# Mixture-of-experts layers: TensorE's work for a pair of experts in three blocks in a fixed order, its sums one pair later

## The chip, the cores and the metric

The kernel runs on one NeuronCore of a Trainium2 chip. Its time is the device time of one launch in microseconds (us), the median over several runs. The profile is of one further execution of the same program.

## The reference

A network of one block and then two layers, on 256 tokens of 1024 numbers. The change touches only the mixture of experts (MoE) that closes each of the two layers. It has 16 experts in 4 groups; each token goes to two experts:

```
p_group = softmax(tok @ w_router_group); grp = argmax(p_group)
top_p, top_i = top_k(softmax(logits of that group's 4 experts), 2)
weight = p_group[grp] * top_p / sum(top_p)
...
for an expert e and its tokens:  y = (silu(tok @ w1[e]) * (tok @ w3[e])) @ w2[e]     # w1, w3: 1024x512, w2: 512x1024
...
x = x + gate * (sum over a token's two experts of weight * y)
```

One layer's weights w1, w3, w2 are 16 x 6 MB = 96 MB in float32; they are read from HBM once per layer.

## The kernel before

The program is written with a tile framework: the code names tiles and operations, and a scheduler decides the order in which each engine takes its instructions, by its own model of their times, unless the code sets it. Each engine then runs its list strictly in order and waits where an operand is not ready.

`moe(layer)` computes a layer's experts in eight **pairs**. Every expert has 64 places for tokens (CAP), so the two experts of a pair share the 128 columns of TensorE's array: expert i=0 uses columns 0 to 63, i=1 columns 64 to 127. A pair's work, with the lines of the kernel before:

- *first products* `ph` (L1644): 32 matmuls on half the columns, c=0 for w1 and c=1 for w3, alternating between the two halves of the array;
- `h` = silu of the first (L1649, ScalarE) times the second (L1664, VectorE), then four transposes to `hT` (L1669), copied out by VectorE and ScalarE (L1671);
- the *combine matrix* `ct` (L1655) and the routing weights `ws` (L1657), from `dm`, which says which token has which place;
- *output products* (L1679): 16 matmuls on half the columns, n=0 and n=1 for the two halves of the 1024 outputs;
- y = output x `ws` x gate (L1696, VectorE), split into a high part `yh` (L1697, ScalarE) and a low part `yl` (L1698, VectorE);
- the *sums* into four accumulators `macc` in PSUM (L1556, in `flush`): eight matmuls on the full array for a pair;
- for every second pair, `dispatch`: two comparisons on VectorE make the next two pairs' `dm` (L1490), and 32 matmuls on the full array (L1496) gather their tokens to `xg`, which ScalarE and VectorE copy out of PSUM (L1502, L1500).

The lines that make a pair's half-array work:

```
for k in range(KC):
    for i in range(2):
        pe.matmul(ps[64 * i:64 * i + 64], xg[:, k, CAP * i:CAP * i + CAP],
                  r3(w[4 * c + 2 * (k // 4) + i], 4)[:, k % 4], start=k == 0, stop=k == KC - 1)
...
fi = [(f, i) for f in range(4) for i in range(2)]
for f, i in sorted(fi, key=lambda v: v[1]) if (pr, n) == (7, 1) else fi:
    pe.matmul(ps[64 * i:64 * i + 64], hT[:, f, 64 * i:64 * i + 64], w2[n][i][:, f], start=f == 0, stop=f == 3)
```

A float32 matmul stands in the trace as two records, so 32 matmuls are 64 records.

Weights come as 1 MB tiles `mw`, twelve to a pair, 96 to a layer, by SP's DMA queue in order. There are 19 places for them; the first 19 of a layer are loaded ahead, during the work before it (L1388), the other 77 as places come free (L1421). Tiles in PSUM come from a pool `pa` of four banks; the other four hold `macc`. Before the last pair stands a branch (`overflow`, L1564 and L1565), which is entered only if an expert has more than 64 tokens; every engine passes it, and nothing of the last pair is ahead of it on TensorE. The last three weight tiles of a layer are issued behind it.

Of the kernel before, what the change touches and what calls it, by code (L numbers as in the profile page):

```python
# [48 lines left out]
def body(tc, A, out, stop=None, start=None):  # L49
# [1375 lines left out]
    def moe(layer):  # L1425
# [5 lines left out]
        def tl(shape, name, bufs=1, dt=F32):  # L1431
            return cur[-1].tile(shape, dt, name=name, tag=name, bufs=bufs)
# [48 lines left out]
        def dispatch(pr):  # L1481

            me, cur[-1] = cur[-1], md
            dm = tl([P, 2, 4, CAP], "dm", dt=F32R)
            xg = tl([P, KC, 4 * CAP], "xg")
            cur[-1] = me
            for i in range(2):
                ready.append((dm.bitcast(F32)[:, :, 2 * i:2 * i + 2], xg[:, :, 2 * CAP * i:2 * CAP * (i + 1)]))
            for b in range(2):
                dve.tensor_tensor(dm[:, b], iota[:, None, 1:CAP + 1].to_broadcast([P, 4, CAP]),  # L1490
                                  po[:, b, 2 * pr:2 * pr + 4, None].to_broadcast([P, 4, CAP]), op=ALU.is_equal)
            for k in range(KC):
                ps = pa([P, 4 * CAP])
                for b in range(2):
                    for x_ in (xnh, xnl):
                        pe.matmul(ps, x_[:, b, k * P:(k + 1) * P], fl(dm[:, b]), start=b == 0 and x_ is xnh,  # L1496
                                  stop=b == 1 and x_ is xnl)
                o = xg[:, k]
                if k % 2:
                    dve.tensor_scalar(o, ps, a[:, k:k + 1], b_[:, k:k + 1], op0=ALU.mult, op1=ALU.add)  # L1500
                else:
                    act.activation(o, ps, AF.Identity, scale=a[:, k:k + 1], bias=b_[:, k:k + 1])  # L1502
                if k == 3:
                    yield
            yield

        ready, md = [], cur[-1]
        xnh, xnl = tl([P, 2, D], "xnh", dt=F32R), tl([P, 2, D], "xnl", dt=F32R)
        for n in range(2):
            ns = slice(512 * n, 512 * n + 512)  # L1510
            for b in range(2):
                act.mul(xnh[:, b, ns], x[:, b, ns], rsx[:, b:b + 1])
                dve.scalar_tensor_tensor(xnl[:, b, ns], x[:, b, ns], rsx[:, b:b + 1], xnh[:, b, ns].bitcast(F32),
                                         op0=ALU.mult, op1=ALU.subtract)
        for _ in dispatch(0):
            pass

        p8 = el.rearrange("p b e g -> p b (e g)").rearrange("p b (s k) -> p b s k", s=2)
        sm, wk = tl([P, 2, 4], "rsm"), tl([P, 2, 2], "wk")
# [9 lines left out]
        wt = tl([P, 2, 16], "wt")  # L1529
        dve.tensor_mul(oe, oe, wk[:, :, :, None].to_broadcast([P, 2, 2, 16]))  # L1530
        dve.tensor_add(wt, oe[:, :, 0], oe[:, :, 1])
        def hy():

            return tl([P, 512], "h")

        def add(b, c, ps, i):

            o = x[:, b, c:c + ps.shape[-1]]
# [10 lines left out]
        def flush():  # L1549

            while late:
                pr, n, ct, ys = late.pop()
                for y_ in ys:
                    for b in range(2):
                        end = pr == 7 - n and y_ is ys[-1]
                        pe.matmul(acc[b][n], ct[:, b * P:(b + 1) * P], y_, start=pr == 0 and y_ is ys[0], stop=end)  # L1556
                        if end:
                            add(b, 512 * n, acc[b][n], n == 0 and 0)
# [69 lines left out]
                                o = x[:, b, 512 * n:512 * n + 512]  # L1628
                                dve.tensor_add(o, o, g_)

        for pr in range(8):
            dm, xg = ready.pop(0)
            nxt = dispatch(pr + 1) if pr % 2 and pr < 7 else iter(())
            w = [mload() for _ in range(8)]
            if pr == 7:
                overflow()
            w2 = [[r3(mload(), 4) for i in range(2)] for n in range(2)]

            ph = []
            for c in range(2):  # L1640
                ps = pa([P, 512], "ph")
# [3 lines that stand above are left out]
                                  r3(w[4 * c + 2 * (k // 4) + i], 4)[:, k % 4], start=k == 0, stop=k == KC - 1)  # L1645
                ph.append(ps)
                if c == 0:
                    h = hy()
                    act.activation(h, ps, AF.Silu)  # L1649
                    flush()  # L1650

                    ps = pa([P, T + 2])
                    d = [fl(dm[:, b]) for b in range(2)]
                    for b in range(2):
                        pe.transpose(ps[:, b * P:(b + 1) * P], d[b], ident)  # L1655
                    for b in range(2):
                        pe.matmul(ps[:, T:T + 2], d[b], wt[:, b, 2 * pr:2 * pr + 2], start=b == 0, stop=b == 1)  # L1657
                    ct, ws = tl([P, T], "ct", dt=F32R), tl([P, 1], "ws", bufs=2)
                    act.copy(ct, ps[:, 0:T])
                    for i in range(2):  # L1660
                        dve.tensor_copy(ws[64 * i:64 * i + 64], ps[64 * i:64 * i + 64, T + i:T + i + 1])
            for j in range(2):
                js = slice(256 * j, 256 * j + 256)
                dve.tensor_mul(h[:, js], h[:, js], ph[1][:, js])  # L1664
            next(nxt, None)
            ps = pa([P, 4, P])
            hT = tl([P, 4, P], "hT")
            for f in range(4):
                pe.transpose(ps[:, f], h[:, f * P:(f + 1) * P], ident)  # L1669
                if f % 2:  # L1670
                    (dve.tensor_copy if f == 1 else act.copy)(hT[:, f - 1:f + 1], ps[:, f - 1:f + 1])  # L1671
            next(nxt, None)

            for n in range(2):
                ps = pa([P, 512])
                fi = [(f, i) for f in range(4) for i in range(2)]

                for f, i in sorted(fi, key=lambda v: v[1]) if (pr, n) == (7, 1) else fi:
                    pe.matmul(ps[64 * i:64 * i + 64], hT[:, f, 64 * i:64 * i + 64], w2[n][i][:, f],  # L1679
                              start=f == 0, stop=f == 3)  # L1680
                if (pr, n) == (7, 1):
                    y = fl(tl([P, 4, P], "hT"))
                    for c in (0, T):
                        cs = slice(c, c + T)
                        dve.scalar_tensor_tensor(y[:, cs], ps[:, cs], ws, gr[:, 512 + c:768 + c], op0=ALU.mult, op1=ALU.mult)  # L1685
                    flush()
                    for c in (0, T):
                        for b in range(2):
                            ps = pa([P, T])
                            pe.matmul(ps, ct.bitcast(F32)[:, b * P:(b + 1) * P], y[:, c:c + T], start=True, stop=True)  # L1690
                            add(b, 512 + c, ps, 1 + c // T)
                    continue
                flush()
                y = hy()
                yh, yl = md.tile([P, 512], F32R, name="yh", tag="yh", bufs=1), tl([P, 512], "yl", dt=F32R)
                dve.scalar_tensor_tensor(y, ps, ws, gr[:, 512 * n:512 * n + 512], op0=ALU.mult, op1=ALU.mult)  # L1696
                act.copy(yh, y)  # L1697
                dve.tensor_sub(yl, y, yh.bitcast(F32))  # L1698
                late.append((pr, n, ct, (yh, yl)))
        esk.close()  # L1700
        esm.close()
        es.close()
# [426 lines left out]
```

## Time and profile before

| | us |
|---|---|
| median of 3 runs | 2102.05 (2101.83 to 2104.94) |
| the profiled execution | 2101.02 |
| its span, first to last instruction | 2099.2 |
| TensorE busy in the span | 1852.7 (88%) |
| MoE of layer 0, first to last product of the pairs | 233.63 |
| MoE of layer 1, the same | 231.52 |

Times below count from the span's start. A row of the timeline gives start, duration, engine (PE is TensorE, DVE VectorE, ACT ScalarE, SPq the DMA queue of SyncE), line, operation, out<-in, shape, count of records, and in brackets how long the engine was idle before it and what ended that. [...] "128\*64" is the part of the array that a matmul uses (rows\*columns).

### The profile page before, as it was taken

Reading aid. Unit: us, or ns where it says so; the run is one execution under the profiler, and the core shown is the slowest. Engines: PE = TensorE matmul, PEld = TensorE weight load, DVE = VectorE, ACT = ScalarE, POOL = GpSimd, SP = SyncE. Lnnn points to the kernel's source line nnn. Section 1 sums busy time; section 2 is a strip of 40 time slices with the busy share of each in tenths; the row PEclk is TensorE's granted clock in tenths of the full one; section 3 lists DMA queues with packets and bytes.
Section 4 is the critical chain, followed back from the end, with each engine's and each line's share of the span. In section 5 each row is a group of like instructions: output and inputs, shape, how many; then the busy total and the mean of one; then the engine's idle time right before and its main releaser. Section 6 shows DMA issues by size and latency. Waiting matters only on the chain. (4 is left out here: it accounts for less than half of the span.)

```text
span 2099.2 us, 27099 instructions
## 1 busy us (share of the span) xinstructions
PE 1852.7 (88%) x9963; PEld 1182.8 (56%) x9963; DVE 1077.3 (51%) x2616; ACT 603.6 (29%) x1232; POOL 448.7 (21%) x407
## 2 busy tenths in 40 slices
PE   7999999989778788787788799979999899989998
PEld 6787897879633233333333398764433699843432
DVE  6635453455857757667665546752112479531212
ACT  4434342344311111212111234721111454311110
POOL 2100000002544444354444200010000255200000
PEclk9999999999899999999898998989999999999999
DMA  9666644845799999999999774059997372669993
GB/s 317 204 231 195 218 139 146 280 153 170 315 427 426 427 427 427 426 409 427 427 426 427 284 285 161 11 201 401 420 419 313 130 281 91 241 246 419 419 420 119
DMA packets 122678, 624.82 MB, mean 298 GB/s; under 512 B 11534, under 2 KB 16494, under 8 KB 65034
## 3 DMA queue, kind: packets, MB, share of 16 engines
q1 hardware_dynamic: 85675, 354.54, 45.5%
q0 software_dynamic: 36864, 268.45, 30.4%
q8 instruction: 83, 1.36, 0.3%
q14 instruction: 56, 0.46, 0.1%
HBM read 621.80 MB, written 1.16 MB: 297 GB/s over the span
## 5 line engine op out<-in xcount | busy, mean ns | idle before, releaser
L986 PE MATMUL acc<-uv,dg 128*128 128x512 f32 x1024 | 495.3, 642 | 125.3 <-ACT dg L984 125.3
L986 PEld LDWEIGHTS acc<-uv,dg 128*128 128x128 f32 x1024 | 205.1, 205 | 413.6 <-issue 240.2
L974 DVE CUSTOM_DVE_ANT_0 uv<-uv,xn 128x1024 f32<-128x1024 f32 x256 | 316.5, 1240 | 204.1 <-DMA uv<-in_puv,ix 199.0
L973 POOL DMA_INDIRECT uv<-in_puv,ix x256 | 286.2, 1118 | 340.4 <-PE acc L986 236.0
L1644 PE MATMUL ph<-mw,xg 128*64 128x512 f32 x1024 | 256.0, 600 | 4.4 <-PEq L1565 2.7
L142 DVE TENSOR_TENSOR wl<-w,wh 128x1024 fp32r<-128x1024 f32 x129 | 162.9, 1266 | 167.7 <-ACT wh L141 110.3
L141 ACT CAST wh<-w 128x1024 fp32r<-128x1024 f32 x166 | 173.4, 1048 | 248.0 <-PE pb L160 73.9
L1644 PEld LDWEIGHTS ph<-mw,xg 128*64 128x64 f32 x1024 | 77.4, 137 | 145.0 <-issue 139.8
L142 POOL TENSOR_TENSOR wl<-w,wh 128x1024 fp32r<-128x1024 f32 x37 | 90.1, 2438 | 243.4 <-PE pa L270 158.3
L980 ACT ACTIVATE ac<-ac 128x4 f32<-128x4 f32 (+1 forms) x65 | 13.3, 205 | 425.7 <-DVE ac L974 425.6
L159 PE MATMUL pa<-xh,wh 128*128 128x256 f32 x480 | 122.1, 291 | 2.1 <-ACT wh L141 2.1
L1679 PE MATMUL pa<-mw,hT 128*64 128x512 f32 x512 | 123.8, 596 | 0.0
L160 PE MATMUL pa<-xl,wh 128*128 128x256 f32 x480 | 120.1, 287 | 0.0
L159 PEld LDWEIGHTS pa<-xh,wh 128*128 128x128 f32 x480 | 93.6, 195 | 6.4 <-ACT wh L141 3.4
L160 PEld LDWEIGHTS pa<-xl,wh 128*128 128x128 f32 x480 | 93.8, 195 | 0.0
L984 ACT ACTIVATE dg<-cf,ac 128x128 f32<-128x128 f32 x256 | 82.6, 390 | 24.7 <-DVE ac L981 20.2
L160 PE MATMUL pb<-xl,wh 128*128 128x256 f32 x352 | 89.5, 289 | 0.0
L159 PE MATMUL pb<-xh,wh 128*128 128x256 f32 x352 | 89.2, 289 | 0.0
L162 PE MATMUL pa<-xh,wl 128*128 128x256 f32 x480 | 69.1, 288 | 19.7 <-POOL wl L142 15.8
L1679 PEld LDWEIGHTS pa<-mw,hT 128*64 128x64 f32 x512 | 38.9, 136 | 69.0 <-issue 68.2
L1696 DVE SCALAR_TENSOR_TENSOR h<-pa,ws,mgr 128x512 f32<-128x512 f32 x30 | 22.5, 751 | 103.6 <-PE pa L1679 102.6
L162 PEld LDWEIGHTS pa<-xh,wl 128*128 128x128 f32 x480 | 62.4, 194 | 22.2 <-POOL wl L142 16.6
(614 smaller groups left out, 2961.9 us busy)
## 6 DMA issues: line engine op xcount, KB each, us to landing
mw<-in_moe_w SPq DMA_DIRECT2D x192, 1024.0 KB, 14.9
awp<-in_ada_w SPq DMA_DIRECT2D x48, 1024.0 KB, 5.5
w<-in_w_in SPq DMA_DIRECT2D x68, 512.0 KB, 4.7
w<-in_hg_c SPq DMA_DIRECT2D x22, 512.0 KB, 3.8
w<-in_wq SPq DMA_DIRECT2D x16, 512.0 KB, 4.3
w<-in_nsa_c SPq DMA_DIRECT2D x16, 512.0 KB, 8.5
w<-in_w_br SPq DMA_DIRECT2D x8, 512.0 KB, 4.2
w<-in_w_out SPq DMA_DIRECT2D x8, 512.0 KB, 3.5
```

The costliest lines, as they stand in the source:

```text
L141: act.copy(wh[:, :n], w[:, :n])
L142: (lo or dve).tensor_sub(wl[:, :n], w[:, :n], wh[:, :n].bitcast(F32))
L159: pe.matmul(ps, wh[:, k], xh[:, k], start=k == 0, stop=False)
L160: pe.matmul(ps, wh[:, k], xl[:, k], start=False, stop=False)
L162: pe.matmul(ps, wl[:, k], xh[:, k], start=False, stop=k == nk - 1)
L973: pool.indirect_dma_start(w, None, A["puv"], bass.IndirectOffsetOnAxis(ap=ix[b][:, k:k + 1], axis=0))
L974: dve.tensor_tensor_reduce(w[:, 0:D], w[:, 0:D], xn[:, b], 1.0, 0.0, ALU.mult, ALU.add, h[:, s:s + 1])
L984: act.mul(dg, ident, hs[:, i:i + 1])
L986: pe.matmul(acc[b][n], dg, w[:, D + 512 * n:D + 512 * n + 512], start=k == 0, stop=k == P - 1)
L1644: pe.matmul(ps[64 * i:64 * i + 64], xg[:, k, CAP * i:CAP * i + CAP], r3(w[4 * c + 2 * (k // 4) + i], 4)[:, k % 4], start=k == 0, stop=k == ...
L1679: pe.matmul(ps[64 * i:64 * i + 64], hT[:, f, 64 * i:64 * i + 64], w2[n][i][:, f], start=f == 0, stop=f == 3)
L1696: dve.scalar_tensor_tensor(y, ps, ws, gr[:, 512 * n:512 * n + 512], op0=ALU.mult, op1=ALU.mult)
```

## The change

Within a pair TensorE's list is now the written order (`manual_schedule` for that engine alone): the 32 first products; then the full-array work, which is the sums of the pair before, the transposes of `h`, `ct` and `ws`, and every second pair all of `dispatch`; then the 16 output products. The other engines are still ordered by the scheduler. The sums of both halves n of a pair wait for the next pair, so `yh` gets two places, and the low part of n=1 uses the place of `hT`. y is made in PSUM, in the bank of the output product, instead of in `h`.

```
-        for _ in dispatch(0):
-            pass
+        dispatch(0)
...
-                pr, n, ct, ys = late.pop()
+                pr, n, ct, ys = late.pop(0)
...
-        for pr in range(8):
-            dm, xg = ready.pop(0)
-            nxt = dispatch(pr + 1) if pr % 2 and pr < 7 else iter(())
-            w = [mload() for _ in range(8)]
-            if pr == 7:
-                overflow()
-            w2 = [[r3(mload(), 4) for i in range(2)] for n in range(2)]
+        def pair(pr, dm, xg, w, w2):
...
                 if c == 0:
-                    h = hy()
+                    h = tl([P, 512], "h")
                     act.activation(h, ps, AF.Silu)
-                    flush()
-
-                    ps = pa([P, T + 2])
...
             for j in range(2):
                 js = slice(256 * j, 256 * j + 256)
                 dve.tensor_mul(h[:, js], h[:, js], ph[1][:, js])
-            next(nxt, None)
+
+            flush()
             ps = pa([P, 4, P])
             hT = tl([P, 4, P], "hT")
             for f in range(4):
                 pe.transpose(ps[:, f], h[:, f * P:(f + 1) * P], ident)
                 if f % 2:
                     (dve.tensor_copy if f == 1 else act.copy)(hT[:, f - 1:f + 1], ps[:, f - 1:f + 1])
-            next(nxt, None)
+
+            ps = pa([P, T + 2])
+            d = [fl(dm[:, b]) for b in range(2)]
+            for b in range(2):
+                pe.transpose(ps[:, b * P:(b + 1) * P], d[b], ident)
+            for b in range(2):
+                pe.matmul(ps[:, T:T + 2], d[b], wt[:, b, 2 * pr:2 * pr + 2], start=b == 0, stop=b == 1)
...
+            if pr % 2 and pr < 7:
+                dispatch(pr + 1)
...
-                flush()
-                y = hy()
-                yh, yl = md.tile([P, 512], F32R, name="yh", tag="yh", bufs=1), tl([P, 512], "yl", dt=F32R)
-                dve.scalar_tensor_tensor(y, ps, ws, gr[:, 512 * n:512 * n + 512], op0=ALU.mult, op1=ALU.mult)
-                act.copy(yh, y)
-                dve.tensor_sub(yl, y, yh.bitcast(F32))
+
+                yh = tl([P, 512], f"yh{n}", dt=F32R)
+                yl = tl([P, 512], "yl", dt=F32R) if n == 0 else fl(tl([P, 4, P], "hT")).bitcast(F32R)
+                dve.scalar_tensor_tensor(ps, ps, ws, gr[:, 512 * n:512 * n + 512], op0=ALU.mult, op1=ALU.mult)
+                act.copy(yh, ps)
+                dve.tensor_sub(yl, ps, yh.bitcast(F32))
                 late.append((pr, n, ct, (yh, yl)))
+
+        for pr in range(8):
+            dm, xg = ready.pop(0)
+            w = [mload() for _ in range(8)]
+            if pr == 7:
+                overflow()
+            w2 = [[r3(mload(), 4) for i in range(2)] for n in range(2)]
+            with tc.manual_schedule(engines={mybir.EngineType.PE}):
+                pair(pr, dm, xg, w, w2)
```

In the kernel after, first products stand at L1631, output products at L1667, the sums at L1548, transposes at L1645, `ct` at L1652, `ws` at L1654, and the branch at L1557.

TensorE's list of the kernel before, from the output products of pair 1 of layer 0 to the middle of pair 2's second first product (numbers at `macc` are buffer numbers):

```order
L1679 MATMUL pa<-mw,hT 64x512 x16
L1644 MATMUL ph<-mw,xg 64x512 x11
L1556 MATMUL macc_10241<-yh,ct 128x512
L1556 MATMUL macc_10243<-yh,ct 128x512
L1644 MATMUL ph<-mw,xg 64x512
L1556 MATMUL macc_10241<-yl,ct 128x512
L1556 MATMUL macc_10243<-yl,ct 128x512
L1644 MATMUL ph<-mw,xg 64x512 x4
L1655 MATMUL pa<-cf,dm 128x128 x2
L1657 MATMUL pa<-wt,dm 128x2 x2
L1644 MATMUL ph<-mw,xg 64x512 x5
```

Here runs of 11, 1, 4 and 5 half-array matmuls alternate with full-array work. The kernel after, the same pair:

```order
L1631 MATMUL ph<-mw,xg 64x512 x32
L1548 MATMUL macc_10241<-yh_10469,ct 128x512
L1548 MATMUL macc_10243<-yh_10469,ct 128x512
L1548 MATMUL macc_10241<-yl,ct 128x512
L1548 MATMUL macc_10243<-yl,ct 128x512
L1548 MATMUL macc_10242<-yh_10483,ct 128x512
L1548 MATMUL macc_10244<-yh_10483,ct 128x512
L1548 MATMUL macc_10242<-hT,ct 128x512
L1548 MATMUL macc_10244<-hT,ct 128x512
L1645 MATMUL pa<-cf,h 128x128 x4
L1652 MATMUL pa<-cf,dm 128x128 x2
L1654 MATMUL pa<-wt,dm 128x2 x2
```

The 32 first products are one run, and everything on the full array stands behind them; the 16 output products follow.

VectorE's list of the kernel before, pair 1 of layer 0, from the comparisons that make the next `dm` to the copies of `xg`:

```order
L1490 TENSOR_TENSOR dm<-cf,pos 128x256 x2
L1661 COPY ws<-pa 64x1 x2
L1664 TENSOR_TENSOR h<-h,ph 128x256 x2
L1500 TENSOR_SCALAR xg<-pa,ma,mod 128x256 x2
L1671 COPY hT<-pa 128x256
L1500 TENSOR_SCALAR xg<-pa,ma,mod 128x256 x2
```

The same place in the kernel after:

```order
L1639 TENSOR_TENSOR h<-h,ph 128x256 x2
L1647 COPY hT<-pa 128x256
L1490 TENSOR_TENSOR dm<-cf,pos 128x256 x2
L1658 COPY ws<-pa 64x1 x2
L1500 TENSOR_SCALAR xg<-pa,ma,mod 128x256 x4
```

The two comparisons have moved from ahead of the product that makes `h` to behind the copy of `hT`, directly ahead of the copies of `xg`.

## Rows read from the trace of the kernel before

**Rows 1.** Windows: MoE of layer 0, two pairs of it, MoE of layer 1

```profile
1412.31:1645.94 233.63, 224.66 (x1002) 88.36 (x1001) 43.01 (x92) 29.61 (x55) 4.68 (x2) 0.99 0.86 351
1487.06:1544.76 57.70, 56.58 (x262) 23.26 (x261) 11.51 (x24) 7.31 (x14) 0.00 (x0) 1.00 1.01 419
1859.19:2090.71 231.52, 222.81 (x1001) 87.01 (x1000) 42.87 (x90) 27.70 (x53) 0.00 (x0) 1.00 0.85 350
```

**Rows 2.** The chain of waits that ended last: start, us, what

```profile
2065.22 13.89 PE ph L1644 x62
```

**Rows 3.** Waits of TensorE in layer 1's MoE: us in total, times, longest

```profile
PE pa L1669 <- DVE h L1664: 3.0, 5, 0.6
PE pa L1669 <- DVE hT L1671: 2.6, 5, 0.5
PE ph L1644 <- DVEq L1565: 1.7, 1, 1.7
PE pa L1496 <- ACT xg L1502: 0.7, 1, 0.7
PE macc L1556 <- ACT yh L1697: 0.7, 1, 0.7
```

**Rows 4.** Timeline of TensorE, layer 0, pair 1's output products to pair 2's

```profile
1458.88 7.09 PE L1679 MATMUL pa<-mw,hT 128*64 128x512 f32 x32
1465.79 5.31 PE L1644 MATMUL ph<-mw,xg 128*64 128x512 f32 x22
1471.04 0.73 PE L1556 MATMUL macc<-yh,ct 128*128 128x512 f32 x2
1471.70 1.07 PE L1644 MATMUL ph<-mw,xg 128*64 128x512 f32 x2
1472.70 0.74 PE L1556 MATMUL macc<-yl,ct 128*128 128x512 f32 x2
...
1475.23 0.44 PE L1655 MATMUL pa<-cf,dm 128*128 128x128 f32 x2
...
1475.94 2.79 PE L1644 MATMUL ph<-mw,xg 128*64 128x512 f32 x10
1478.66 0.73 PE L1556 MATMUL macc<-yh,ct 128*128 128x512 f32 x2
...
1479.79 5.36 PE L1644 MATMUL ph<-mw,xg 128*64 128x512 f32 x22
1485.76 0.41 PE L1669 MATMUL pa<-cf,h 128*128 128x128 f32 x2 [0.60 <-DVE h L1664]
1486.69 0.44 PE L1669 MATMUL pa<-cf,h 128*128 128x128 f32 x2 [0.52 <-DVE hT L1671]
1487.06 3.65 PE L1679 MATMUL pa<-mw,hT 128*64 128x512 f32 x16
```

**Rows 5.** Timeline of TensorE: matmuls of dispatch, back to back

```profile
1457.01 0.28 PE L1496 MATMUL pa<-dm,xnl 128*128 128x256 f32 x1
1457.13 0.28 PE L1496 MATMUL pa<-dm,xnh 128*128 128x256 f32 x1
```

**Rows 6.** The line of the comparisons for `dm`: ns min/median/max, first and last start

```profile
L1490 DVE TENSOR_TENSOR dm<-cf,pos x16: 417/418/425, 1406.2 to 2000.7; 128x256 fp32r<-128x256 f32 x16
```

**Rows 7.** Timeline of TensorE behind the branch in layers 0 and 1, and pair 7's output

```profile
1614.45 1.28 PE L1644 MATMUL ph<-mw,xg 128*64 128x512 f32 x2 [2.67 <-PEq L1565]
...
2062.43 1.04 PE L1644 MATMUL ph<-mw,xg 128*64 128x512 f32 x2 [1.75 <-DVEq L1565]
...
2081.00 9.71 PE L1679 MATMUL pa<-mw,hT 128*64 128x512 f32 x32
```

**Rows 8.** Windows: layer 0, behind the branch

```profile
1615.00:1622.00 7.00, 7.00 (x20) 3.35 (x20) 1.50 (x4) 0.37 (x1) 0.00 (x0) 0.51 0.97 375
```

**Rows 9.** Timeline of the DMA queue: the streamed weight tiles of layer 0

```profile
1415.99 200.40 SPq L1421 DMA_DIRECT2D mw<-in_moe_w  x77
```

**Rows 10.** Lines of layer 1's MoE: xg's copies (busy us, mean ns, idle before)

```profile
L1502 ACT ACTIVATE xg<-pa,mod,ma 128x256 f32<-128x256 f32 x13 | 7.2, 563 | 18.6 <-PE ph L1644 9.6 <-PE pa L1496 9.0
```

## What the change should do to the time

> **What bounds the kernel now.** I read the windows first. Layer 0's experts take 233.63 us, layer 1's 231.52, together 22% of the span, and TensorE is busy in 224.66 and 222.81 us of them [rows 1]. The end of the chain of waits is matmuls of the last pair [rows 2]. TensorE's waits in layer 1 sum to 8.7 us, those in front of the transposes being the largest [rows 3]. So TensorE sets the pace. The weight stream does not quite: twelve tiles of 1.049 MB to a pair at 419 GB/s are 30.0 us, and two pairs take 57.70, so TensorE eats tiles a little faster than they come, out of the 19 loaded ahead [rows 1].
>
> Busy is not full, and that is what the timeline is for. 32 records (16 half-array matmuls) of output products take 1465.79 - 1458.88 = 6.91 us: 0.432 us each, because the two experts run side by side, 0.864 for two. The single first product at 1471.70 holds the engine until 1472.70: 1.00 us, with nothing on the other half [rows 4]. It counts as busy all the same. Runs of 11, 1, 4 and 5 between full-array work, as the order shows, leave a half empty at each odd end.
>
> **The change part by part.**
>
> *Unit prices, all from [rows 4] unless said.* First products in one run: 32 x 0.432 = 13.8 us. Output products: 6.9. Sums: two of them between half-array work take 1471.70 - 1471.04 = 0.66, four take 1479.79 - 1478.66 = 1.13, so one costs 0.235 and the change to the full array and back 0.19; eight in a row with one change are 2.07. Transposes with the wait for the first copy of hT: 1487.06 - 1485.76 = 1.30. ct and ws: 1475.94 - 1475.23 = 0.71, less the change 0.52. Dispatch: 32 x 0.12 = 3.84 [rows 5].
>
> *What goes.* The wait for the product h, 0.60 in front of the transposes: the eight sums now stand there, 2.07 us, and the two products and their start are 0.6 us behind the last first product, so the cover is ample. It stays in pair 0, which has no sums before it. The odd ends go, six in two pairs by the order (each costs the empty half, 0.43), and seven of nine changes there and back, at 0.19.
>
> *What stays.* The wait between the transposes, 0.52: the second two share a PSUM tile with the copy of the first two. Before, dispatch hid it in odd pairs; now every pair pays it. The branch: 2.67 and 1.75 us before [rows 7]; I take 2.2. Pair 7's last output product keeps its order one expert after the other: 9.71 us instead of 7.09 [rows 7, 4], so 2.6 more.
>
> *What comes.* One new wait, in the three odd pairs of a layer that dispatch. The comparisons for the new dm overwrite what the ws matmuls have just read, so they can't start before these, and dispatch needs them. Before, they lay under first products and nobody waited for them. Each takes 0.42 [rows 6]. From below the wait is 0.42, if the first matmuls need only the first comparison; from above about 1.3, two in a row and a copy ahead of them in VectorE's queue. Dispatch's first two matmuls (0.24) can cover part of the second, so I take 0.8. Behind the comparisons on VectorE stand the ws copies and its copies of xg; nobody needs those within dispatch's own 3.84 us.
>
> *Hidden.* y, yh and yl are read out of PSUM, one step after another, while 13.8 us of the next pair's first products run; a bank of the pool comes round four tiles later, so those products take the banks of hT and ct, not of y. If that cover were gone, two steps of about 0.7 us (yh waited for 0.7 once, [rows 3]) would stand in each pair. The new place of yl, in hT, is free since the output products have read hT, and the next hT is written behind the sums. The weight queue's order is the same.
>
> *The sum for a layer.* Pair 0: 13.8 + 0.6 + 1.30 + 0.7 + 6.9 = 23.3. An even pair: 13.8 + 2.07 + 1.30 + 0.52 + 6.9 = 24.6. An odd pair with dispatch: 24.6 + 3.84 + 0.8 = 29.2, so two pairs 53.8 for 57.70. Pair 7: 24.6 + 2.6 = 27.2. Layer: 23.3 + 3 x 29.2 + 3 x 24.6 + 27.2 + 2.2 = 214.1 us. Against 231.52 layer 1 gains 17.4. Layer 0 would gain 19.5, but 7 us of its 233.63 ran at 0.51 of the clock, at the lower level of 1.2 GHz, behind the 2.67 us in front of the branch [rows 8, 7]; that is 3.4 us, and since a gap of that kind stays, I leave one such drop in and count 16.1. Together 33.5. What follows layer 0 starts as much earlier, and the last additions at the end do the same work: 0.
>
> A check by differences: six odd ends 2.6 and seven changes 1.3, less 0.7 for waits (1.12 before, 1.04 + 0.8 after), are 3.2 us for two pairs, against 3.9 by the sum. With 3.2 the layers give 28 together. I keep 33.
>
> The profiled execution took 2101.02 us, its span 2099.2; the median of the runs is 1.0 above the first. **2102 - 33 = 2069 us.**
>
> **One rule against it.** If only the change of shape cost anything and a half-empty array did not, seven changes at 0.19 less the 0.7 of waits would be 0.6 us for two pairs, some 5 us in all: 2097. The lone matmul of 1.00 us against 0.43 speaks against that. [...]
>
> **The rivals.**
>
> *The clock falls in each pair (slower).* The full-array block now holds the transposes, a wait of 0.52, small matmuls and in odd pairs a wait of 0.8, all at one place, between two dense runs. [...] Against it: the even pairs of before had 0.60 and 0.52 with only transposes between them, and the clock stood at 1.00 over two such pairs [rows 4, 1]. [...]
>
> *The weight stream takes over.* Two pairs need 60 us of stream and would take 53.8. The stream of layer 0 starts at 1416 [rows 9]; its 73rd tile, the last first-product tile of pair 7, is there at about 1416 + 73 x 2.50 = 1598.5 plus the few us that a start takes, say 1603. TensorE would ask for it at 1412.3 + 184.7 + 2.2 + 10.3 = 1609.5. That leaves 6 us. The last three tiles are issued behind the branch, at about 1599, and are asked for from 1616 on. If the stream lost 10 us in each layer, the gain would shrink by 4 each: 2077.
>
> *Late operands.* In a fixed order every operand that is late stops everything. If dispatch, crowded with copies, waits 3 us instead of 0.8 (for banks or for VectorE), six times, the gain falls by 13: 2082. For it: the 0.7 that dispatch once waited for a copy of xg [rows 3]. Against it: a copy takes ScalarE 0.56 us [rows 10], and it has every second one, so one for each 0.96 us of gathering.
>
> *It does nothing.* If scheduler and hardware had in fact overlapped the halves across the breaks, only waits would differ, and by the 0.7 they get worse: 2107. The same row of 1.00 us speaks against it.
>
> **How the numbers follow.** Forecast (2060 to 2077, the clock drops and the dispatch wait within their bounds) 0.72; stream 0.07; late operands 0.09; only the changes of shape count 0.03; nothing, at the upper edge of what counts as the same (within 0.2%, 4 us, about what a measurement of this kernel can tell from no change), 0.05; clock 0.04. The low end is no clock drop at all (-3.4) and the dispatch wait at 0.42 (-2.3), and a little for small waits that vanish: 2060. The high end has drops in both layers (+3.4), the late operands at 13: 2084. Faster is the sum of the first four, 0.91; the fifth is split, so same 0.03, slower 0.06.
>
> **What would show it.** In the trace after, two pairs should be 53.8 us apart; the first products of a pair one row of 64 records in 13.8; eight sums in 2.1; the wait for h only in pair 0; 0.52 between the transposes eight times in a layer; a wait of dispatch for the comparisons, 0.8, three times. The layers should be 214 to 218 us long and the DMA share between 0.9 and 1. I am wrong if first products wait for DMA in pair 7, if the clock is below 1.00 away from the branch, or if the pairs are 57 us apart with the runs unbroken.

## The result, and the profile after

The changed kernel took 2074.40 us (median of 4 runs, 2069.25 to 2081.53), the kernel before 2101.94 on the same chip: a ratio of 0.9858, 95% interval 0.9831 to 0.9884. The forecast was 2069 (2060 to 2084), faster. Run again later, the same kernel took 2067.17 (2064.94 to 2075.62, 5 runs), ratio 0.9846 (0.9823 to 0.9869). The profile below is that of the slowest run, 2081.53, span 2079.7; the profile of the repeat, 2064.94, has the same expert layers, and most of the difference lies in one earlier stage, told at the end.

The windows of both expert layers and of two pairs between them, as in [rows 1] (the stretch A:B and its length in us, then busy time and records of TensorE, its weight loads, VectorE, ScalarE and GpSimd, TensorE's granted clock as a share of full speed, the busy share of the DMA engines, GB/s):

```profile
1424.99:1642.47 217.48, 206.79 (x1002) 87.68 (x1001) 43.95 (x91) 29.69 (x55) 2.69 (x2) 0.99 0.91 377
1495.23:1549.02 53.79, 52.24 (x262) 22.80 (x261) 11.63 (x24) 7.30 (x14) 0.00 (x0) 1.00 1.01 420
1855.06:2072.22 217.16, 206.80 (x1002) 87.73 (x1001) 43.97 (x91) 27.80 (x53) 0.00 (x0) 0.99 0.90 373
```

Layer 0 went from 233.63 to 217.48 us, layer 1 from 231.52 to 217.16, two pairs from 57.70 to 53.79. TensorE does the same matmuls in 16 to 18 us less busy time, which is where the gain is; what is not busy grew, by less than 2 us. Over the two pairs the granted clock is 1.00 and the DMA engines are busy throughout (1.01, 420 GB/s); TensorE has no wait for a weight tile in either layer.

The timeline of TensorE in an even pair of layer 1, to hold against [rows 4]:

```profile
1900.74 7.09 PE L1667 MATMUL pa<-mw,hT 128*64 128x512 f32 x32
1907.66 13.90 PE L1631 MATMUL ph<-mw,xg 128*64 128x512 f32 x64
1921.49 0.74 PE L1548 MATMUL macc<-yh,ct 128*128 128x512 f32 x2
1922.07 0.63 PE L1548 MATMUL macc<-yl,ct 128*128 128x512 f32 x2
1922.54 0.62 PE L1548 MATMUL macc<-yh,ct 128*128 128x512 f32 x2
1923.00 0.62 PE L1548 MATMUL macc<-hT,ct 128*128 128x512 f32 x2
1923.46 0.38 PE L1645 MATMUL pa<-cf,h 128*128 128x128 f32 x2
1924.36 0.44 PE L1645 MATMUL pa<-cf,h 128*128 128x128 f32 x2 [0.52 <-DVE hT L1647]
```

One row of 64 records from start to start takes 1921.49 - 1907.66 = 13.83 us, 0.432 for two; the eight sums 1.97; the wait for `h` is gone and 0.52 between the transposes is left. TensorE's waits in layer 1, which answer to [rows 3] (us in total, times, longest):

```profile
PE pa L1645 <- DVE hT L1647: 4.9, 8, 1.3
PE ph L1631 <- DVEq L1557: 3.3, 1, 3.3
PE pa L1496 <- DVE dm L1490: 1.6, 3, 0.5
PE pa L1645 <- DVE h L1639: 0.6, 1, 0.6
```

`h` is waited for once (pair 0), `hT` in each pair, `dm` in the three pairs that dispatch. Two of these are larger than forecast: the gap at the branch, and one wait for `hT` of 1.3 us. Both belong to pair 7, here in layer 0:

```profile
1613.46 15.65 PE L1631 MATMUL ph<-mw,xg 128*64 128x512 f32 x64 [3.57 <-DVEq L1557]
...
1632.69 0.44 PE L1645 MATMUL pa<-cf,h 128*128 128x128 f32 x2 [1.32 <-DVE hT L1647]
```

Pair 7 waits 3.57 us at the branch, its first products take 15.65 instead of 13.9, and the second transposes wait 1.32 instead of 0.52. The slower first products are explained by a window right behind the branch, where the granted clock is 0.50 for 3.42 us (1.71 us lost, of 15.65 - 13.90 = 1.75):

```profile
1614.15:1617.57 3.42, 3.42 (x10) 1.20 (x8) 0.00 (x0) 0.00 (x0) 0.00 (x0) 0.50 1.01 405
```

### The profile page after: what moved, and what is told of

Read it like the earlier page. It is cut to its first block, busy times and chain, and to the rows that moved or that the text cites. A ratio compares the mean times of both kernels' runs of the same rounds, so it can differ in the third digit from the quotient of the medians.

```text
span 2079.7 us, 27097 instructions
## 1 busy us (share of the span) xinstructions
PE 1833.2 (88%) x9963; PEld 1191.3 (57%) x9963; DVE 1075.7 (52%) x2616; ACT 603.9 (29%) x1232; POOL 449.4 (22%) x407
## 5 line engine op out<-in xcount | busy, mean ns | idle before, releaser
L1631 PE MATMUL ph<-mw,xg 128*64 128x512 f32 x1024 | 226.0, 600 | 6.8 <-DVEq L1557 6.8
L1631 PEld LDWEIGHTS ph<-mw,xg 128*64 128x64 f32 x1024 | 76.1, 138 | 153.3 <-issue 152.2
L1667 PE MATMUL pa<-mw,hT 128*64 128x512 f32 x512 | 116.9, 595 | 0.0
L1639 DVE TENSOR_TENSOR h<-h,ph 128x256 f32<-128x256 f32 x32 | 12.0, 418 | 200.5 <-PE ph L1631 200.5
L1667 PEld LDWEIGHTS pa<-mw,hT 128*64 128x64 f32 x512 | 36.7, 137 | 67.1 <-issue 66.2
```

## The experiments

**The spread.** First the changed kernel once more, with nothing edited.

> The changed kernel once more. Its four runs so far were 2081.5, 2069.3, 2078.5 and 2070.4 us, and its profiled run (2081.5) showed the granted clock at half speed for 6.8 us four times between 320 and 375 us, in a stage that the change does not touch. Theory: two levels, near 2070 and near 2080, told apart by that stage; a profile near 2070 shows 320:375 some 10 us shorter, and 217 us in each expert layer as before. Rival: the spread lies in the expert layers, and they then differ by some 5 us each between a run near 2070 and one near 2080.

Its five runs went from 2064.94 to 2075.62 us. The profiled one (2064.94) has layers of 217.48 and 217.19 us, those of the changed kernel's profile within 0.03, and between 320 and 375 us it is 11 us shorter. So most of the spread is that stage's, as the first theory had it, and the rest lies in other stages ahead of the experts: layer 0 starts 16.0 us earlier in this profile. The two levels are less sharp than the theory said. Its windows stand in the last section.

**Do odd ends cost, and what does a break cost?** Two kernels spread the eight sums among the first products of the next pair, each alone, seven more breaks in each pair from 1 on; only the places differ:

```diff
+            sums = one_by_one()
             ...
                         pe.matmul(ps[64 * i:64 * i + 64], xg[:, k, CAP * i:CAP * i + CAP], ...
+                        if 16 * c + 2 * k + i + 1 in (4, 8, 12, 16, 20, 24, 28, 32):   # even
+                        if 16 * c + 2 * k + i + 1 in (3, 8, 11, 16, 19, 24, 27, 32):   # odd
+                            next(sums, None)
             ...
-            flush()
+            for _ in sums:
+                pass
```

> The changed kernel with the eight sums of a pair no longer in one block, but one behind each four first products (runs of 4, seven more breaks in each of seven pairs of a layer). Theory of the prediction: each break costs a change, 0.19 us, so 9.3 us a layer, and the sums no longer cover the wait for h, 0.4 to 0.6 in seven pairs, 3 to 4 us a layer: a layer takes 230 us, the kernel some 24 us more than the changed kernel. Rival, changes cost nothing: only the waits, 220 us a layer, 6 to 8 us more.

> The same as the one with even runs, the same number of breaks and sums, but behind first products 3, 8, 11, 16, 19, 24, 27 and 32, so that the runs are 3, 5, 3, 5 ... long. Theory: each odd end leaves half the array empty for 0.43 us; eight runs in each of seven pairs are 24 us a layer more than with even runs, 48 us for the kernel. Rival, the hardware pairs half products across a break, or an idle half costs nothing: the time of the kernel with even runs within 3 us. Rival, only every second odd end costs (3 and 5 together make whole pairs): 24 us.

Even runs: 2107.59 us (2105.70 to 2118.14), ratio to before 1.0023 (1.0005 to 1.0040). Odd runs: 2155.22 (2153.23 to 2169.81), ratio 1.0267 (1.0232 to 1.0303). The odd ends are right: 47.6 us between the medians of the two, 48 expected. Since the times spread by more than 10 us, the layers are the firmer witness. Layer 1 with even and with odd runs takes 236.51 and 261.25 us, 24.7 more for 24 expected:

```profile
1872.31:2108.82 236.51, 225.39 (x1002) 82.24 (x1001) 43.87 (x91) 27.75 (x53) 0.00 (x0) 0.99 0.83 342
```

```profile
1886.49:2147.74 261.25, 250.28 (x1002) 92.04 (x1001) 43.92 (x91) 27.78 (x53) 0.00 (x0) 0.99 0.76 310
```

In the timeline one even run, and one pair of odd runs:

```profile
1897.93 1.94 PE L1644 MATMUL ph<-mw,xg 128*64 128x512 f32 x8
1899.80 0.51 PE L1559 MATMUL macc<-yh,ct 128*128 128x512 f32 x1
1900.24 1.94 PE L1644 MATMUL ph<-mw,xg 128*64 128x512 f32 x8
```

```profile
1915.25 1.93 PE L1644 MATMUL ph<-mw,xg 128*64 128x512 f32 x6
1917.11 0.50 PE L1559 MATMUL macc<-yl,ct 128*128 128x512 f32 x1
1917.54 2.79 PE L1644 MATMUL ph<-mw,xg 128*64 128x512 f32 x10
1920.26 0.51 PE L1559 MATMUL macc<-yl,ct 128*128 128x512 f32 x1
```

Three half products (6 records) take 1917.11 - 1915.25 = 1.86 us, as long as four (1899.80 - 1897.93 = 1.87); five take 2.72. In these runs the odd one cost as much as two.

The breaks were priced too low: 40 us over the changed kernel's 2067 instead of 24. Four half products are 4 x 0.432 = 1.73, but a run of them takes 1.87, and a lone sum 0.43 instead of 0.235. So a break there and back cost 0.14 behind the half-array work and 0.20 behind the full-array work here, 0.34 in all. The 0.19 of the prediction was the second part alone. Were it that a lone sum is dear, pairs of sums would be cheap:

```diff
-                        if 16 * c + 2 * k + i + 1 in (4, 8, 12, 16, 20, 24, 28, 32):
-                            next(sums, None)
+                        if 16 * c + 2 * k + i + 1 in (8, 16, 24, 32):
+                            next(sums, None), next(sums, None)
```

> The sums of a pair two by two, behind first products 8, 16, 24 and 32: three more breaks in seven pairs of a layer, all runs even, two sums in each. Theory of the prediction: 0.19 us a break, 4 us a layer, 221.5 us. Rival, what the kernel with single sums showed, 0.38 us a break: 8 us a layer, 225.5 us. Between them, if a lone sum is dearer than one in a group: near the first.

It took 2084.26 us (2080.79 to 2090.53), ratio 0.9910 (0.9876 to 0.9945). Layers 226.07 and 225.65 us: a break cost the higher price also with two sums in it. An even pair takes 25.77 for 24.55, three breaks of 0.41. So the price of a break is 0.34 by the single rows and up to 0.41 by whole pairs.

**What is owed to the fixed order, and what to the sums coming later?** The order in which the code of before is written, made fixed for TensorE (one fixed stretch for pairs 0 to 6, one for pair 7; an edit of the kernel before):

```diff
-        for pr in range(8):
+        def old_pair(pr):
...
             if pr == 7:
                 overflow()
+                block.enter_context(tc.manual_schedule(engines={mybir.EngineType.PE}))
...
+        block = ExitStack()
+        with tc.manual_schedule(engines={mybir.EngineType.PE}):
+            for pr in range(7):
+                old_pair(pr)
+        with block:
+            old_pair(7)
```

> The order of work of the kernel before as its code is written (first products 16, sums 4 and ct, first products 16, dispatch in two halves around the transposes, sums of the first half behind the output products), but fixed for TensorE, so that all runs of half products have an even length; the sums of the first half of y are not put off. Theory of the prediction (odd run ends at 0.43 us and changes at 0.19 us are what was won): two pairs take 53.8 plus five more changes (0.95) plus one wait for h (0.6) = 55.3 us; a layer 223 us; 10 to 14 us over the changed kernel, 20 us under the kernel before. Rival, putting off the sums is what won: near 57.7 us for two pairs, as before, and near 2100 us. Rival, only that the order is fixed matters and shape changes cost nothing: 53.8 and the time of the changed kernel.

2082.92 us (2075.83 to 2087.86), ratio 0.9902 (0.9881 to 0.9924). Its two pairs and layer 1:

```profile
1857.38:2078.54 221.16, 210.35 (x1002) 84.86 (x1001) 43.55 (x91) 28.13 (x53) 0.00 (x0) 0.99 0.89 366
1882.27:1937.41 55.14, 53.23 (x261) 22.22 (x261) 11.50 (x24) 7.40 (x15) 0.00 (x0) 1.00 1.01 420
```

55.14 for 55.3 expected. Two thirds of the 3.91 us that two pairs gain come with a fixed order of even runs, without the blocks; the blocks bring the rest.

The blocks with the sums behind their own pair's output products instead of one pair later:

```diff
                 late.append((pr, n, ct, (yh, yl)))
+            if pr < 7:
+                flush()
...
+        block = ExitStack()
+        block.enter_context(tc.manual_schedule(engines={mybir.EngineType.PE}))
...
             if pr == 7:
+                block.close()
                 overflow()
+                block.enter_context(tc.manual_schedule(engines={mybir.EngineType.PE}))
...
-            with tc.manual_schedule(engines={mybir.EngineType.PE}):
-                pair(pr, dm, xg, w, w2)
+            pair(pr, dm, xg, w, w2)
+        block.close()
```

The fixed order is here one stretch over pairs 0 to 6 and one over pair 7, where the changed kernel has one for each pair.

> The changed kernel with the eight sums in the block behind the output products of their own pair (pairs 0 to 6), in fixed order, so not put off by a pair. Theory: the output products and first products stay whole, but TensorE waits for y: the sums are eight by 0.235 and end 0.7 us later for the last of the arithmetic, one change more, and the wait for h, 0.6, is back in pairs 1 to 7; at the branch 2 us are given back, since the arithmetic is done by then. That is 8.4 us a layer, 226 us, 17 us more than the changed kernel. Rival, putting the sums off is worth nothing once the runs are whole: 217 us a layer. Rival, TensorE waits for the whole of y and its parts (2.2 us in each pair), or the clock falls at each such wait: 236 us a layer or more.

2099.20 us (2095.78 to 2102.36), ratio 0.9974 (0.9956 to 0.9992): nearly the whole gain is lost. TensorE's waits in layer 1:

```profile
PE pa L1645 <- DVE h L1639: 4.9, 8, 0.6
PE ph L1631 <- PEq L1557: 4.6, 1, 4.6
PE pa L1645 <- DVE hT L1647: 4.1, 8, 0.5
PE macc L1548 <- ACT yh L1685: 2.9, 7, 0.4
```

The wait for `h` is back in every pair, `yh` is waited for in seven, and a break more is paid: an even pair takes 26.49 instead of 24.55. I had 1.5 of these 1.9 us; the rest is the dearer break and the part of the wait for the low half that the trace doesn't set apart. The layer is 231.92 and not 226 partly for this, and partly because the branch did not get 2 us shorter but 1.3 longer: TensorE stands idle for 4.56 us there instead of 3.26, put down to its own queue. (From output products to first products it is 7.57 us, but that holds the eight sums and their wait; the changed kernel pays its sums in pair 7.) Of the 14.8 us that the layer loses, 13.5 are in the pairs and 1.3 at the branch. So putting the sums off is what made blocks pay here.

**Without a fixed order**, the changed program left to the scheduler:

```diff
-            with tc.manual_schedule(engines={mybir.EngineType.PE}):
-                pair(pr, dm, xg, w, w2)
+            pair(pr, dm, xg, w, w2)
```

> The changed kernel's program with TensorE's order left to the scheduler. Its order keeps most blocks, puts the dm transposes between the transposes of h, and splits a few runs oddly (25 and 7, 1). Theory: what the fixed order buys is only the whole runs, so this is within 5 us of the changed kernel, some 4 us a layer gained at the transposes and some given back at the splits. Rival, the order fixed by hand is what gains: near the kernel before, 2090 to 2100 us.

2085.98 us (2078.13 to 2089.07), ratio 0.9923 (0.9906 to 0.9941); neither. In pairs 1 and 2 it is better than the fixed order, 52.23 us for the two. It loses later, by split runs and by sums put in front of the branch, where TensorE waits for `yh` and then for the branch (layer 1):

```profile
PE macc L1548 <- PEq L1557: 4.0, 1, 4.0
PE pa L1645 <- DVE h L1639: 2.4, 4, 0.6
PE macc L1548 <- ACT yh L1685: 2.2, 2, 1.5
```

**The wait between the transposes.** In the scheduler's order `dm`'s transposes stand between `h`'s. Done by hand:

```diff
                 if f % 2:
                     (dve.tensor_copy if f == 1 else act.copy)(hT[:, f - 1:f + 1], ps[:, f - 1:f + 1])
+                if f == 1:
+                    pc = pa([P, T + 2])
+                    d = [fl(dm[:, b]) for b in range(2)]
+                    for b in range(2):
+                        pe.transpose(pc[:, b * P:(b + 1) * P], d[b], ident)
...
-            ps = pa([P, T + 2])
-            d = [fl(dm[:, b]) for b in range(2)]
...
```

> The two transposes of dm and the products for ws go between the second and the third transpose of h, where TensorE waits 0.52 us for the copy of hT in each pair (1.32 us in pair 7). Theory that the wait is covered: 16 x 0.52 = 8.3 us, and a part of the 0.52 us that odd... even pairs wait for dm, so 8 to 10 us under the changed kernel, some 4.5 us for each expert layer. Rival, the wait only moves: ScalarE now does the copy to ct ahead of the second copy of hT, and the output products wait for that; no change, or 0.2 us a pair more (3 us slower).

2059.11 us (2057.45 to 2059.45), ratio 0.9793 (0.9774 to 0.9812), 8.1 us under the changed kernel in the same comparison; the layers 212.98 and 212.69, two pairs 52.27. In layer 1:

```profile
PE ph L1631 <- DVEq L1557: 3.3, 1, 3.3
PE pa L1645 <- DVE hT L1647: 0.8, 1, 0.8
PE pa L1645 <- DVE h L1639: 0.6, 1, 0.6
```

Seven of eight waits for `hT` are gone, and those for `dm` with them: its comparisons now run beside `h`'s last transposes. These waits were 5.7 us in layer 1, and the layer gains 4.5: behind the branch pair 7's first products take 16.83 us instead of 15.65, 1.2 more, and the mean granted clock of the layer is 0.98 instead of 0.99. What is left, 0.8, is pair 7's. There VectorE does its two additions to `x` (0.68 each) ahead of the copy that TensorE waits for. Put behind it:

```diff
-                            add(b, 512 * n, acc[b][n], n == 0 and 0)
+                            adds.append((b, 512 * n, acc[b][n], n == 0 and 0))
...
+            while adds:
+                add(*adds.pop(0))
...
-            with tc.manual_schedule(engines={mybir.EngineType.PE}):
+            with tc.manual_schedule(engines={E.PE, E.DVE} if pr == 7 else {E.PE}):
```

> The transposes of dm between the second and third transpose of h, as before, and besides in pair 7 the two additions to x behind the copy of hT on VectorE. Theory: the 0.76 us that pair 7 still waited there go, 1.5 us under the kernel with the first edit alone, and as fast as that (2057 to 2059) or 2055 to 2058 us. Rival: the additions that are late hold the last sums' banks, and the end of each layer gets longer by up to 1.3 us; no change.

2055.35 us (2054.50 to 2057.44), ratio 0.9777 (0.9758 to 0.9795), the fastest kernel that computes all. The layers take 211.99 and 211.97 us, 0.7 to 1.0 less; no wait for `hT` is left.

**The branch.** Without it:

```diff
-            if pr == 7:
-                overflow()
```

> Leaves out the overflow branch (with these inputs it is never taken). Theory: TensorE's 3.4 us gap at the branch is VectorE's arithmetic on the second half of pair 6, which the branch makes all engines end first, and the clock falls for 3.4 us because of that gap. Then the gap falls under 0.7 us, the first products of pair 7 go from 15.65 to 13.9 us, and each layer loses 4.4 us: 8 to 9 us in all. Rival: the clock falls for another reason (pair 7's place in the layer, its transfers), then only the gap is won, 5 to 5.5 us. Rival, something else holds pair 7 (its operands): under 2 us.

2059.59 us (2054.54 to 2060.50), ratio 0.9786 (0.9765 to 0.9807). The gap is 0, pair 7's first products take 13.90 (in layer 0 at a granted clock of 1.00), the layers 211.94 and 211.97, 5.5 and 5.2 us less:

```profile
1593.61 7.09 PE L1667 MATMUL pa<-mw,hT 128*64 128x512 f32 x32
1600.52 13.90 PE L1631 MATMUL ph<-mw,xg 128*64 128x512 f32 x64
```

So both gap and clock belong to the branch. That VectorE's arithmetic is what makes it long is not shown by this, since everything went at once. A try to shorten that arithmetic, by halves:

```diff
+                for cs in ([slice(0, T), slice(T, 2 * T)] if (pr, n) == (6, 1) else [slice(0, 512)]):
...
-                dve.scalar_tensor_tensor(ps, ps, ws, gr[:, 512 * n:512 * n + 512], op0=ALU.mult, op1=ALU.mult)
-                act.copy(yh, ps)
+                    dve.scalar_tensor_tensor(ps[:, cs], ps[:, cs], ws, gr[:, g], op0=ALU.mult, op1=ALU.mult)
+                    act.copy(yh[:, cs], ps[:, cs])
```

> The kernel with both edits (dm transposes moved, additions of pair 7 behind the copy), and in pair 6 the second y, yh and yl in two halves of 256 columns, so that VectorE and ScalarE work side by side and VectorE comes to the branch sooner. Theory: VectorE's chain of 2.16 us takes some 1.6, the gap at the branch goes from 3.57 and 3.25 to about 3.0 and 2.7, 1 us under the kernel with both edits. Rival: four more instructions cost as much as the overlap gives; no change.

A miss: 2059.27 us (2055.94 to 2065.75), ratio 0.9789 (0.9762 to 0.9816), and the gap went up, to 4.03 and 3.71 us. VectorE's second half waited 0.49 us for ScalarE to have read the first (one tile of PSUM), so the chain took 1593.85 - 1591.18 = 2.67 us instead of 2.16: 0.51 more, and the gap 0.46 more. That VectorE comes last is shown by it. What stands behind VectorE, a last kernel told, which leaves the subtraction out:

```diff
-                dve.tensor_sub(yl, ps, yh.bitcast(F32))
-                late.append((pr, n, ct, (yh, yl)))
+                low = (pr, n) != (6, 1)
+                if low:
+                    dve.tensor_sub(yl, ps, yh.bitcast(F32))
+                late.append((pr, n, ct, (yh, yl) if low else (yh,)))
```

> The changed kernel, but pair 6's second half has no low part yl: VectorE's subtraction of 0.69 us ahead of the branch and two of the eight sums of pair 7 are left out (the output loses the low bits of that half). What ends last at the branch: in the changed kernel VectorE's last word comes at 1613.19 us and the first product starts 0.25 us behind it, while TensorE's own branch instruction ends at 1612.61 and would let it start some 0.4 us later, at 1613.05. Theory A, VectorE alone holds the gap: without the subtraction and its wait (1.4 us) it falls from 3.57 and 3.25 to about 2.2 and 1.9 us. Theory B, TensorE's own branch instruction, 5.9 to 6.2 us from the moment its queue comes to it, stands right behind: the gap falls by only 0.4 us, to about 3.15 us in layer 0, and the clock still drops behind it. Pair 7's sums get 0.5 us shorter in both.

One run, 2075.31 us. First products of pair 7 in layer 1:

```profile
2039.13 13.95 PE L1631 MATMUL ph<-mw,xg 128*64 128x512 f32 x64 [2.94 <-PEq L1557]
```

The gap is 3.38 in layer 0 and 2.94 in layer 1, 0.19 and 0.32 less, and now it is TensorE's own queue that is named. Theory B. The rows of the branch in the changed kernel say why (PEldq is TensorE's queue, DVEq VectorE's; xcount, ns min/median/max, first and last start):

```profile
L1557 PEldq COMPARE_BRANCH  x2: 5938/6074/6210, 1606.7 to 2036.4; - x2
...
L1557 DVEq COMPARE_BRANCH  x2: 63/68/72, 1612.6 to 2042.4; - x2
```

TensorE's branch instruction took 5.94 and 6.21 us here, VectorE's 0.06 and 0.07. TensorE's queue comes to it at 1606.7, ahead of the array, which has work until 1609.9, and is through at 1612.6; VectorE comes to its own at 1612.6 too. TensorE's is not a wait for VectorE: with the sums in their own pair, TensorE took 3.84 us for it, and VectorE had long done its own:

```profile
L1557 PEldq COMPARE_BRANCH  x2: 3835/3842/3850, 1615.1 to 2057.8; - x2
L1557 DVEq COMPARE_BRANCH  x2: 63/68/72, 1615.8 to 2058.5; - x2
```

So in the changed kernel two things end almost together, VectorE's arithmetic last. The kernels with spread sums tell them apart. With even runs TensorE's instruction was short and over at 1623.5 + 3.3 = 1626.9 in layer 0, 2.6 us before VectorE came to its own, and the gap was the changed kernel's all the same, 3.57 and 3.25:

```profile
L1569 PEldq COMPARE_BRANCH  x2: 3318/3614/3910, 1623.5 to 2070.9; - x2
L1569 DVEq COMPARE_BRANCH  x2: 63/68/72, 1629.5 to 2076.8; - x2
```

Why VectorE comes later than before is to be read in its list. VectorE in layer 1, before and after:

```profile
2060.72 0.75 DVE L1696 SCALAR_TENSOR_TENSOR h<-pa,ws,mgr 128x512 f32<-128x512 f32 x1 [4.40 <-PE pa L1679]
2062.27 0.69 DVE L1698 TENSOR_TENSOR yl<-h,yh 128x512 fp32r<-128x512 f32 x1 [0.80 <-DVEq L1565]
```

```profile
2040.01 0.76 DVE L1684 SCALAR_TENSOR_TENSOR pa<-pa,ws,mgr 128x512 f32<-128x512 f32 x1 [1.27 <-PE pa L1667]
2041.48 0.69 DVE L1686 TENSOR_TENSOR hT<-pa,yh 128x512 fp32r<-128x512 f32 x1 [0.71 <-ACT yh L1685]
```

Before, the branch (L1565) stood between `y` and the subtraction, so only `y` was ahead of it. Now it stands behind both, and the subtraction has to wait for ScalarE: it starts 1.47 us behind `y`. From the end of the output products to the start of pair 7's first products there are 1.75 us before and 3.26 after, 1.51 more. No kernel moved the branch alone.

TensorE's instruction took some ninety times as long as VectorE's. No run here shows what TensorE's queue waits for, nor why its instruction took 3.3 to 3.9 us in some cases (3.32 and 3.69 in the kernel before) and 6 in others; the kernel left to the scheduler has both, 5.94 in layer 0 and 3.67 in layer 1. The clock stayed up behind the gap of 2.94 us in the kernel without the subtraction (first products 13.95 us, granted clock 1.00 from 2042.30 to 2049.30). It fell behind that kernel's 3.38 (15.65 us, 0.76 from 1610 to 1617) and behind the changed kernel's 3.57 and 3.26 (15.65 us each, down to 0.50). But it also fell for 7 us behind 2.67 in [rows 7, 8], to 0.51, where other work stood around it, so by these runs the gap's length alone doesn't decide it.

## Why the prediction was right, step by step

- **What bounds it**: TensorE, with a half-empty array that counts as busy. Right: 222.81 us of busy time became 206.80 with the same matmuls, though a little more of them at the slow clock (0.99 in the mean of layer 1, 1.00 before). The stream kept up, 420 GB/s over two pairs and no wait of TensorE for a weight tile.
- **Odd ends, 0.43 each, six in two pairs**: right, 0.42 by the two kernels with spread sums. First products of two pairs take 27.67 us from start to start instead of 31.33, 3.66 less, added up over their records: six ends are 2.6, and seven breaks by 0.14 are 1.0 of the other 1.1.
- **Changes at 0.19**: mis-sized. There and back is 0.34. The missing 0.14 stood in [rows 4]: the lone product took 1.00 us, not 2 x 0.432. What was summed by blocks came out right all the same (pair 1 29.24 for 29.2, pair 2 24.55 for 24.6, two pairs 53.79 for 53.8), since blocks hold their own changes. The check by differences, 3.2, was off by this and by the waits, though not by this alone: with 0.34 for each of seven changes and 0.43 for waits it would be 4.5, and 3.91 was measured. The full-array work itself got only 0.6 us shorter in two pairs, where seven times 0.20 are 1.4; what it loses again inside the block is not set apart.
- **Waits**: the one for `h` goes and stays in pair 0, 0.62; 0.52 between the transposes is paid by all. Right. Pair 7's is the exception, 1.32. Dispatch waits 0.52, not 0.8, three times: its first product needs one comparison, which is near the lower bound of 0.42. The waits of two pairs grow by 0.43 instead of 0.7.
- **Hidden work**: `y`, `yh` and `yl` are waited for nowhere but at the branch. That this needs the delay of a pair is shown by the kernel without it, 13.5 us a layer of waits and breaks and 1.3 more at the branch.
- **The branch, 2.2 us**: the step that failed. It is 3.57 and 3.26. I took the mean of [rows 7] as if it were a fixed price, though two different things end there: TensorE's own queue in layer 0, behind four sums that covered a part of its 3.3 us, and VectorE in layer 1. I did not ask what would stand ahead of the branch in VectorE's list. There the subtraction and its wait came ahead of it, 1.5 us. Without them it would not have been 2.2 us either: TensorE's own instruction, now 6 us, left 3.38 and 2.94.
- **Pair 7, +2.6**: two things more. The clock drop comes in both layers (1.8 us each) and not in layer 0 alone (3.4), and the copy of `hT` comes behind two additions (0.8). The forecast names the lower level in GHz, which no run shows; they show 0.51 of full speed in [rows 8] and 0.50 behind the branch of the changed kernel.
- **The sum**: layer 0 gained 16.1, as predicted, though by other terms: gap, drop and the late copy 3.57 + 1.8 + 0.8 less 0.8 for dispatch are 5.4, against 2.2 + 3.4 = 5.6. Layer 1 gained 14.3 and not 17.4. The stretch behind the last output product got 1.0 us shorter (7.5 for 8.5), and the start of what follows layer 0 1.2, which I had at 0. Together 32.6 us, for 33. That these come so near is in part luck: the branch, the drop in layer 1 and the late copy cost nearly 6 us that I did not have, and a smaller drop in layer 0, dispatch's shorter waits and the two stretches made up for them. The medians differ by 27.5 us, and by 35.1 with the repeat, since stages that the change does not touch vary by more than the error of the sum.
- **The rivals**: clock in each pair (1.00 over the two pairs), stream and late operands are excluded by the rows above; changes of shape alone and no effect by the odd runs.

## What to carry to other kernels

When two half-array products run side by side, count the runs between full-array work: here each odd end cost a whole product more (0.43 us) and each break 0.34 to 0.41, and all of it was booked as busy. Ask of a block order whether what the block needs was finished long before: here the sums had to come a pair later (217.16 us for layer 1, 231.92 with the sums in their own pair). Of a branch, read what stands ahead of it in each engine's list and how long each queue's own branch instruction takes, not only who came last.

## What was not expected

The granted clock falls in a stage that no kernel here touches, in some executions and not in others. The same stretch in the profiled run of the changed kernel (2081.53 us), and in that of its repeat (2064.94 us):

```profile
320.00:375.00 55.00, 55.00 (x275) 39.54 (x273) 14.98 (x44) 9.08 (x23) 0.00 (x0) 0.75 0.30 102
```

```profile
320.00:375.00 55.00, 55.00 (x364) 41.08 (x363) 17.90 (x47) 14.02 (x30) 0.53 (x1) 0.97 0.43 145
```

TensorE is busy throughout in both, but 275 records fit where 364 did: the granted clock is 0.75 in the mean of the first and 0.97 of the second. In the first it is 0.50 in four stretches, from 324 to 330, 338 to 344, 355 to 361 and 369 to 375 us. The work of this stretch costs 11 us more, and the expert layers of the two runs agree within 0.03 us. The order of TensorE's instructions is the same. Ahead of the first fall stand single small products that alternate, 0.43 us by the record for each two (here of the slower run):

```profile
322.67 0.43 PE L678 MATMUL pa<-qd,sn 128*128 128x64 f32 x2
323.03 0.43 PE L679 MATMUL pa<-it,vn 64*128 64x64 f32 x2
...
323.76 0.57 PE L679 MATMUL pa<-it,vn 64*128 64x64 f32 x2
324.12 2.02 PE L684 MATMUL pa<-vn,kd 64*128 64x128 f32 x8
```

The repeat has the same alternating rows, and the row of L684 behind them took 1.11 us there instead of 2.02. What decides whether the clock falls stays open. It means that changes of under 10 us in this kernel have to be read from the stage that they touch, not from a few times.
